# The modulation's product in column groups on TensorE, and attention steps as contiguous groups with the two heads alternating

## The chip, the core and the metric

The kernel runs on one core of one Trainium2 chip. The time is the device time of one execution in microseconds (us). Engines are named as in the profile: PE (TensorE, with its weight loads as PEld), DVE (VectorE), ACT (ScalarE), POOL (GpSimd) and SP (SyncE, which here only issues DMAs).

## What is computed

256 tokens of width 1024 pass through two hybrid layers, then through one block with modulation, two kinds of attention and a mixture of 32 experts. Cut to what matters here:

```python
for l in range(2):                                   # hybrid layers, all in float32
    h = rmsnorm(x, norm_g); proj = h @ w_in          # 1024 x 11168
    y_a = conv(...)                                  # a short causal convolution, gated
    q = (rmsnorm(c_q) @ w_uq); kv = (rmsnorm(c_kv) @ w_ukv)   # c_q 256 wide, c_kv 128 wide
    y_b = causal_attention(q, k, v) * silu(b_z)      # "mla": 8 heads
    y_c = dilated_attention(dq, dk, dv) * silu(c_z)  # "dil": 8 heads of 64, 3 groups of windows
    x = x + (g_a*(y_a @ w_out_a) + g_b*(y_b @ w_out_b) + g_c*(y_c @ w_out_c)) @ w_o

mod_x = silu(c) @ w_ada + b_ada                      # w_ada: 1024 x 6144, 25 MB
mod_c = silu(c_ctx) @ w_ada + b_ada
sh1, sc1, gt1, sh2, sc2, gt2 = split(mod_x, 6)       # of mod_c only the first two are used
h  = rms_norm(x) * (1 + sc1) + sh1                   # likewise hc from ctx with mod_c
x  = x + gt1 * (concat(gqa(h, hc), diff(h, hc)) @ w_o)   # gqa: 8 heads of 64, diff: 4 pairs of heads of 64
x  = x + gt2 * moe(rms_norm(x) * (1 + sc2) + sh2)    # 32 experts, top 4 of each token
out = rms_norm(x)
```

The modulation depends on `c` and `c_ctx` alone, so it can be worked out at any time before the second block.

## The kernel before

**Stages.** Up to some 800 us the two hybrid layers run, then the second block's attention and the router (`second`), and from about 1030 us the experts, whose 384 loads of 1 MB fill the DMA engines. All projections are float32 products made of three products of split operands (`mm3`, L180 to L182): a weight chunk of 128x4x512 (1 MB, `raw`) comes over SP's queue (L164) into a ring of three buffers with the tag `raw`; ACT makes the high part `wh` (L156), DVE the low part `wl` = `raw` − `wh` (L158); PE then multiplies the activations' parts `hh` and `hl` (or `Y`) with them. A ring buffer is free again when its `wl` is made.

**Side work.** Everything that is not a projection is written as generators: `ada` (the modulation), `mla_prep`, `mla_att`, `dil_att`, context, `gqa`, `diff`. At every weight chunk `pump` (L70) steps each generator by its rate in the table `RT` and gives its instructions the priority offset of the table `HI`. From priorities and its own estimate of time the framework's scheduler then sets the order in which each engine gets its instructions; each engine works through its own list in order, and waits at an instruction whose operand isn't there.

**The modulation (`ada`, L776).** 24 column chunks of 256, each in two halves of 512 rows: a DMA of 512 KB issued by POOL (L818), for each half. For `c`, POOL multiplies all 128x1024 numbers with silu(c) (L828) and adds them up in steps (L830, L832, L835, L836). For `c_ctx`, in the first eight chunks, DVE multiplies and adds 128x256 numbers at a time (L824, L827). What is left is summed over the 128 partitions by products with a column of ones on PE (L794 for the first eight chunks, L803 for the others). The results are `modT` (columns) and `modr` (rows).

**The attention steps.** A unit is two heads and one block of 128 queries; `pipe` alternates the first step of a unit with the second of the one before. The first makes scores for one head after the other on 64 rows of PE each (`dil` L669: three products per head of 256, 128 and 128 columns; `gqa` L958 and `diff` L986: one of 512), then the softmax; the second transposes the probabilities (`transp_p`, L599) and multiplies them with the values (L647, L684, L970, L994). In `mla_prep`, the inverse roots of four columns `css` come from `rsqrt`, eleven DVE instructions (L117 to L122). `mla_heads` scales the 128x768 queries and keys first on DVE (L478), then on POOL (L479), before rotating a part of them (L484 to L487).

## Time and profile before

| | |
|---|---|
| median of 3 runs | 1975.49 us (1973.59 to 1976.54) |
| profiled execution | 1972.42 us, its span 1970.7 us |
| PE busy | 1913.1 us (97% of the span) |
| DVE busy | 915.2 us (46%) |
| ACT busy | 615.8 us (31%) |
| POOL busy | 403.3 us (20%) |
| mean granted PE clock | 0.982 |
| DMA, mean over the span | 289 GB/s |

Busy shares are means over stages with different limits. POOL's work lies wholly ahead of the experts, and DVE's nearly so. A row of the timeline has the start, the time, the engine, the line, the output and inputs by name, the shape, the number of instructions merged in the row, and, in brackets, how long the engine stood idle ahead of it and what ended that. A float32 product shows as two instructions, its two passes. `128*64` ahead of a shape is the tile of PE that the product uses (rows*columns).

### The profile page before, as it was taken

To read this page: it belongs to the slowest core of one execution; us is meant where nothing else is said; L and a number is where in the kernel's file an instruction comes from. 1 tells how busy PE (TensorE), PEld (TensorE's weight loads), DVE (VectorE), ACT (ScalarE), POOL (GpSimd) and SP (SyncE) were. 2 spreads that over 40 slices of the span, in tenths; PEclk is the share of its full clock that TensorE was granted. 3 is DMA by queue.
4 is the path that set the end of the run, shared out by engine and by line. 5 is a ranking of instruction groups with operands and counts; after the bars stand their busy time and mean duration, and the time that the engine had idled before them with its cause. 6 is when DMAs were issued, how large, how long until landed. Compare 5 with 4: busy or idle time off the path is not lost. (4 is left out here: it accounts for less than half of the span.)

```text
span 1970.7 us, 25935 instructions
## 1 busy us (share of the span) xinstructions
PE 1913.1 (97%) x10349; PEld 1184.5 (60%) x10349; DVE 915.2 (46%) x1728; ACT 615.8 (31%) x1109; POOL 403.3 (20%) x325
## 2 busy tenths in 40 slices
PE   8989999989899999999999999999999998999997
PEld 6878988978679889886663333333333333333332
DVE  6898777588976675888671101111111011111111
ACT  4646445446465454465550000000000000100001
POOL 3125436663435334512020000000000000000000
PEclk8989999999899999999999999999999998999999
DMA  6544545546446444654469999999999999999997
GB/s 222 195 142 162 189 147 168 193 172 221 164 161 213 162 132 161 214 185 140 160 238 400 420 381 421 420 421 421 420 421 421 421 421 420 420 421 420 421 421 289
DMA packets 138452, 568.59 MB, mean 289 GB/s; under 512 B 10603, under 2 KB 16747, under 8 KB 90198
## 3 DMA queue, kind: packets, MB, share of 16 engines
q1 hardware_dynamic: 129664, 540.69, 71.0%
q0 software_dynamic: 6912, 25.17, 3.7%
q8 instruction: 83, 1.36, 0.3%
q10 hardware_dynamic: 1750, 1.03, 0.2%
q14 instruction: 43, 0.35, 0.1%
HBM read 565.79 MB, written 1.05 MB: 288 GB/s over the span
## 5 line engine op out<-in xcount | busy, mean ns | idle before, releaser
L158 DVE TENSOR_TENSOR wl<-raw,wh 128x1024 fp32r<-128x1024 f32 (+3 forms) x255 | 338.4, 1330 | 125.9 <-ACT wh L156 121.9
L156 ACT ACTIVATE wh<-raw 128x1024 fp32r<-128x1024 f32 (+3 forms) x255 | 263.0, 1035 | 226.5 <-PE mm L181 204.0
L1388 ACT ACTIVATE modr<-g 128x512 f32<-128x512 f32 x32 | 20.2, 630 | 654.4 <-DVE g L1387 654.4
L182 PE MATMUL mm<-hh,wl 128*128 128x256 f32 x768 | 220.6, 289 | 0.0
L181 PE MATMUL mm<-hl,wh 128*128 128x256 f32 x768 | 220.2, 287 | 0.0
L180 PE MATMUL mm<-hh,wh 128*128 128x256 f32 x768 | 219.8, 287 | 0.0
L1387 DVE TENSOR_SCALAR g<-mm 128x512 f32<-128x512 f32 x32 | 22.1, 692 | 407.5 <-PE mm L1377 407.5
L129 POOL TENSOR_TENSOR rm<-ss,mhalf 128x1 f32<-128x1 f32 x10 | 6.3, 631 | 959.9 <-DVE ss L128 958.0
L181 PE MATMUL mm<-wl,hh 128*128 128x512 f32 (+2 forms) x424 | 170.8, 403 | 12.0 <-DVE wl L158 12.0
L182 PE MATMUL mm<-wh,hl 128*128 128x512 f32 (+2 forms) x424 | 169.9, 401 | 2.1 <-DVE hl L216 1.3
L180 PE MATMUL mm<-wh,hh 128*128 128x512 f32 (+2 forms) x424 | 163.0, 406 | 6.8 <-ACT hh L248 3.7
L828 POOL TENSOR_TENSOR araw<-araw,tb 128x1024 f32<-128x1024 f32 x48 | 104.5, 2176 | 297.2 <-DVE part L824 123.8
L182 PEld LDWEIGHTS mm<-hh,wl 128*128 128x128 f32 x768 | 144.3, 189 | 6.4 <-issue 4.4
L180 PEld LDWEIGHTS mm<-hh,wh 128*128 128x128 f32 x768 | 144.9, 189 | 4.7 <-issue 4.2
L181 PEld LDWEIGHTS mm<-hl,wh 128*128 128x128 f32 x768 | 144.8, 188 | 3.4 <-issue 2.0
L1444 DVE TENSOR_TENSOR ys<-kaT,mm 128x512 f32<-128x512 f32 x16 | 11.0, 688 | 276.7 <-PE mm L1464 266.4
L181 PEld LDWEIGHTS mm<-wl,hh 128*128 128x128 f32 x424 | 84.6, 199 | 29.2 <-DVE wl L158 14.7
L180 PEld LDWEIGHTS mm<-wh,hh 128*128 128x128 f32 x424 | 84.1, 200 | 28.0 <-ACT hh L248 5.4
L182 PEld LDWEIGHTS mm<-wh,hl 128*128 128x128 f32 x424 | 84.2, 199 | 20.1 <-DVE hl L249 2.1
L830 POOL TENSOR_TENSOR araw<-araw 128x512 f32<-128x512 f32 x48 | 83.9, 1748 | 3.6
L1377 PE MATMUL mm<-mr,xT 128*64 128x512 f32 x328 | 77.8, 603 | 0.4 <-DMA mr<-in_w_in_dram 0.4
L1365 PEld LDWEIGHTS mm<-modr,vb 128*128 128x128 f32 x512 | 63.6, 206 | 14.4 <-issue 13.0
(450 smaller groups left out, 3579.4 us busy)
## 6 DMA issues: line engine op xcount, KB each, us to landing
raw<-in_w_in_dram SPq DMA_DIRECT2D x84, 1024.0 KB, 5.4
mr<-in_w_in_dram SPq DMA_DIRECT2D x41, 1024.0 KB, 18.2
mw<-in_w_in_dram SPq DMA_DIRECT2D x39, 1024.0 KB, 19.8
mv<-in_w_in_dram SPq DMA_DIRECT2D x27, 1024.0 KB, 19.8
mY<-in_w_in_dram SPq DMA_DIRECT2D x26, 1024.0 KB, 19.8
araw<-in_w_ada_dram POOLq DMA_DIRECT2D x48, 512.0 KB, 4.4
mw<-in_w_out_dram SPq DMA_DIRECT2D x21, 1024.0 KB, 19.2
mr<-in_w_out_dram SPq DMA_DIRECT2D x19, 1024.0 KB, 19.8
```

The lines of the kernel that those rows point to most:

```text
L156: nc.scalar.activation(wh, src, AF.Copy)
L158: eng.tensor_tensor(wl, src, wh.bitcast(F32), op=ALU.subtract)
L180: nc.tensor.matmul(out, sh, mh, start=first, stop=False, skip_group_check=skip)
L181: nc.tensor.matmul(out, sh, ml, start=False, stop=False, skip_group_check=skip)
L182: nc.tensor.matmul(out, sl, mh, start=False, stop=last, skip_group_check=skip)
L828: nc.gpsimd.tensor_tensor(raw, raw, cT[:, 0, kh * 4:kh * 4 + 4, None].to_broadcast([128, 4, 256]), op=ALU.mult)
L830: nc.gpsimd.tensor_tensor(raw[:, 0:2], raw[:, 0:2], raw[:, 2:4], op=ALU.add)
L1365: nc.tensor.matmul(p[:, j], self.h2[:, t, k * 128:(k + 1) * 128], sx[:, t].rearrange("p e c -> p (e c)"), start=(t == 0 and j == 0), stop= ...
L1377: mm = self.nc.tensor.matmul(hp[i][h * 64:h * 64 + 64], xT[:, k, cols], w[:, o:o + 512], start=False, stop=(k == 7))
L1387: nc.vector.tensor_scalar(g, hg, 7.0, None, op0=ALU.min)
L1388: nc.scalar.activation(th, g, AF.Tanh, scale=0.851)
L1444: nc.vector.tensor_tensor(ys[:, h], gt2[h], yp[h], op=ALU.mult)
```

## The change

**`ada`.** The weights come in 24 loads of 128x2048 (1 MB) by SP's queue, into the ring of the projections' chunks (the same tag and three buffers). Each load is multiplied on PE with a stationary operand of 128x32, whose first two columns are silu(c) and silu(c_ctx) and the others zero, in four products of 512 columns, each in its own group of 32 columns of PE. DVE adds the result out of PSUM to what is there (ACT copies the first). After a third, four transposes turn the first 2048 columns into `modT`. POOL's and DVE's products with the weights, the sums by ones and the column `one` go. The rate falls from 0.437 to 0.235 steps per chunk.

**Groups.** `group()` raises the priority by 400 around the transposes of `transp_p`, the products with the values and the scores, so that the scheduler keeps them together. In `dil`, `gqa` and `diff`, scores of both heads go to two PSUM tiles taken at once, with the heads alternating, so that neighbours use different halves of PE's rows.

**Two small ones.** `mla_prep` makes its inverse roots by one power on POOL; only half of `modr` is cleared at the start.

```diff
-RT = {"ada": 0.437, ...}
+RT = {"ada": 0.235, ...}
+GROUP = 400
+    def group(self):
+        return self.tc.high_priority(offset=GROUP)
...
     def mla_prep(self, l, ps):
+        r = tmp.tile([128, 4], F32, name="cr", tag="cr", bufs=1)
+        nc.gpsimd.tensor_tensor(r, css, self.mhalf, op=ALU.pow)
         yield
-        r = self.rsqrt(tmp, css, 4, "c")
...
     def transp_p(self, p, nb):
-        for j in range(nb):
-            nc.tensor.transpose(ps[:, j, :], p[:, j * 128:(j + 1) * 128], self.ident)
+        with self.group():
+            for j in range(nb):
+                nc.tensor.transpose(ps[:, j, :], p[:, j * 128:(j + 1) * 128], self.ident)
...
     def dil_att(self, l):
         def first(pr, t):
+            ss = [self.at_ps([128, 512]) for _ in range(2)]
+            with self.group():
+                for g, o, n in cols[t]:
+                    for e in range(2):
+                        es = slice(e * 64, (e + 1) * 64)
+                        nc.tensor.matmul(ss[e][:, o:o + n], self.qT[g][es, pr, ts],
+                                         self.kT[g][es, pr, ts if g else slice(0, 256)], start=True, stop=True)
             for e in range(2):
-                s = self.at_ps([128, 512])
-                for g, o, n in cols[t]:
-                    nc.tensor.matmul(s[:, o:o + n], self.qT[g][es, pr, ts], ...)
...
     def ada(self):
+        cS = A.tile([128, 8, 32], F32, name="cS", tag="cS")
+        acc = A.tile([128, 512], F32, name="aacc", tag="aacc")
+        for r in range(3):
+            dst = acc if r == 0 else self.modr[:, r - 1]
+            for kk in range(8):
+                raw = self.ring.tile([128, 2048], F32, name="araw", tag="raw")
+                nc.sync.dma_start(raw, d["w_ada"][kk * 128:(kk + 1) * 128, r * 2048:(r + 1) * 2048])
+                p = self.at_ps([128, 512])
+                with self.group():
+                    for j in range(4):
+                        nc.tensor.matmul(p[32 * j:32 * j + 32], cS[:, kk, :], raw[:, j * 512:(j + 1) * 512],
                                          start=True, stop=True)
+                if kk:
+                    nc.vector.tensor_tensor(dst, dst, p, op=ALU.add)
+                else:
+                    nc.scalar.activation(dst, p, AF.Copy)
+                yield
+            if r == 0:
+                columns()
+                yield
-        for c in range(24):
...
-                nc.gpsimd.dma_start(raw, d["w_ada"][kh * 512:(kh + 1) * 512, c * 256:(c + 1) * 256]
-                                    .rearrange("(k p) n -> p k n", p=128))
...
-                            nc.vector.scalar_tensor_tensor(parts[1], raw[:, k, :], cT[:, 1, kk:kk + 1], parts[1],
-                                                           op0=ALU.mult, op1=ALU.add)
...
-                nc.gpsimd.tensor_tensor(raw, raw, cT[:, 0, kh * 4:kh * 4 + 4, None].to_broadcast([128, 4, 256]),
-                                        op=ALU.mult)
-                nc.gpsimd.tensor_tensor(raw[:, 0:2], raw[:, 0:2], raw[:, 2:4], op=ALU.add)
```

**What it moves, in the engines' orders.** A row has the line, the instruction, output and inputs (a number behind a name is that of the buffer), the output's shape, and a count where rows repeat. The lines after the change are shifted: L180 to L182 become L184 to L186, L669 becomes L673, L164 L168, L479 L483.

PE before, at the first dilated scores of the first layer, between projection products of 256 columns:

```order
L182 MATMUL mm<-Y_99,wl 128x256
L180 MATMUL mm<-Y_99,wh 128x256
L669 MATMUL at<-kT_169,qT_166 128x128
L181 MATMUL mm<-Y_99,wh 128x256
L669 MATMUL at<-kT_170,qT_167 128x128
L182 MATMUL mm<-Y_99,wl 128x256
```

PE after, at the same unit, with a group of the modulation (L821) ahead of it:

```order
L821 MATMUL at<-araw,cS 32x512 x4
L673 MATMUL at<-kT_168,qT_165 128x256 x2
L673 MATMUL at<-kT_169,qT_166 128x128 x2
L673 MATMUL at<-kT_170,qT_167 128x128 x2
L184 MATMUL mm<-hh,wh 128x256
L185 MATMUL mm<-hl,wh 128x256
```

The scores of this unit, scattered one by one before, now stand in pairs of the two heads (x2). PE after, at the next unit, some 15 rows on:

```order
L184 MATMUL mm<-hh,wh 128x256
L673 MATMUL at<-kT_169,qT_166 128x128
L673 MATMUL at<-kT_170,qT_167 128x128
L673 MATMUL at<-kT_168,qT_165 128x256
L185 MATMUL mm<-hl,wh 128x256
L186 MATMUL mm<-hh,wl 128x256
```

Here the three products of one head stand together, but without the other head's between them, and projections follow.

POOL before, around `mla_heads` of the second layer:

```order
L818 DMA araw<-in_w_ada_dram 128x4x256
L828 TENSOR_TENSOR araw<-araw,tb 128x1024
L830 TENSOR_TENSOR araw<-araw 128x512
L479 TENSOR_TENSOR Vd<-Vd,tb 128x768 x4
L832 TENSOR_TENSOR part_5569<-araw 128x256
L818 DMA araw<-in_w_ada_dram 128x4x256
```

POOL after, the same place, from the layer's first norm (L130):

```order
L130 TENSOR_TENSOR rm<-ss,mhalf 128x1 x2
L427 TENSOR_TENSOR cr<-css,mhalf 128x4
L483 TENSOR_TENSOR Vd<-Vd,tb 128x768 x4
L506 MEMSET u 128x4x2
L832 MEMSET brow 128x1024
```

The modulation's instructions are gone from POOL, and the power of `mla_prep` (L427) stands ahead of the four products.

SP before, in the first layer:

```order
L164 DMA raw<-in_w_ukv_dram 128x512
L164 DMA raw<-in_w_in_dram 128x4x512 x17
L164 DMA raw<-in_w_out_b_dram 128x4x512
L164 DMA raw<-in_w_in_dram 128x4x512 x2
L164 DMA raw<-in_w_out_b_dram 128x4x512
```

SP after, the same stretch, up to the last of these 17 chunks but one:

```order
L168 DMA raw<-in_w_ukv_dram 128x512
L168 DMA raw<-in_w_in_dram 128x4x512 x3
L817 DMA araw<-in_w_ada_dram 128x2048
L168 DMA raw<-in_w_in_dram 128x4x512 x5
L817 DMA araw<-in_w_ada_dram 128x2048
L168 DMA raw<-in_w_in_dram 128x4x512 x4
L817 DMA araw<-in_w_ada_dram 128x2048
L168 DMA raw<-in_w_in_dram 128x4x512 x4
L817 DMA araw<-in_w_ada_dram 128x2048
```

A load of the modulation's weights now stands between every two to six chunks of the projections, in the same queue and the same ring.

## Rows read from the trace of the kernel before

**Rows 1.** Windows: stretch, width, busy PE, PEld, DVE, ACT, POOL; clock, DMA, GB/s

```profile
0.00:50.00 50.00, 40.75 (x192) 32.81 (x193) 33.51 (x60) 21.56 (x40) 16.62 (x27) 0.83 0.67 224
...
100.00:150.00 50.00, 43.44 (x198) 35.42 (x197) 46.63 (x105) 23.25 (x36) 15.93 (x10) 0.90 0.43 137
...
400.00:450.00 50.00, 44.84 (x240) 37.08 (x240) 41.69 (x47) 23.18 (x40) 29.30 (x23) 1.00 0.53 181
...
500.00:550.00 50.00, 42.16 (x192) 34.73 (x191) 45.14 (x96) 23.62 (x33) 14.13 (x6) 0.90 0.49 162
...
1200.00:1900.00 700.00, 691.58 (x3116) 266.00 (x3114) 94.42 (x154) 45.86 (x84) 0.00 (x0) 0.99 1.01 421
```

**Rows 2.** Timeline of all engines from 502 to 518 us

```profile
502.50 2.73 POOL L828 TENSOR_TENSOR araw<-araw,tb 128x1024 f32<-128x1024 f32 x1 [3.21 <-DMA araw<-in_w_ada_dram]
...
503.39 1.89 DVE L122 SCALAR_TENSOR_TENSOR rs_y<-rs_t,rs_y 128x32 f32<-128x32 f32 x1
...
505.31 1.32 DVE L120 SCALAR_TENSOR_TENSOR rs_t<-rs_y 128x32 f32<-128x32 f32 x1
...
507.81 6.80 DVE L478 TENSOR_TENSOR Vd<-Vd,rs_y 128x768 f32<-128x768 f32 x4
...
514.53 2.82 DVE L158 TENSOR_TENSOR wl<-raw,wh 128x1024 fp32r<-128x1024 f32 x1
...
517.40 0.80 PE L181 MATMUL mm<-wl,hh 128*128 128x512 f32 x1 [7.37 <-DVE wl L158]
```

**Rows 3.** Timeline of all engines from 37 to 42 us

```profile
37.87 1.88 POOL L828 TENSOR_TENSOR araw<-araw,tb 128x1024 f32<-128x1024 f32 x1 [6.19 <-DVE rs_t L120]
...
37.89 1.89 DVE L121 TENSOR_TENSOR rs_t<-rs_t,css 128x4 f32<-128x4 f32 x1
...
39.81 0.16 DVE L122 SCALAR_TENSOR_TENSOR rs_y<-rs_t,rs_y 128x4 f32<-128x4 f32 x1
...
41.40 0.45 PE L432 MATMUL at<-ident,G 128*128 128x128 f32 x1 [3.25 <-DVE G L427]
```

**Rows 4.** Timeline of all engines from 423 to 427 us

```profile
423.63 0.57 POOL L129 TENSOR_TENSOR rm<-ss,mhalf 128x1 f32<-128x1 f32 x1 [9.17 <-DVE ss L128]
...
424.18 1.88 POOL L828 TENSOR_TENSOR araw<-araw,tb 128x1024 f32<-128x1024 f32 x1
424.23 2.38 DVE L227 TENSOR_SCALAR XM<-x,rm 128x1024 f32<-128x1024 f32 x1 [0.69 <-POOL rm L129]
...
426.76 0.41 PE L243 MATMUL at<-ident,XM 128*128 128x128 f32 x2 [1.82 <-DVE XM L227]
```

**Rows 5.** Waits of PE, longest in total: us, times, longest

```profile
PE mm L181 <- DVE wl L158: 12.0, 4, 7.4
```

**Rows 6.** Timeline of PE from 961 to 1032 us

```profile
961.62 1.98 PE L986 MATMUL mm<-kbT,G 64*128 64x512 f32 x6
963.53 1.08 PE L1164 MATMUL at<-rt,sT 128*128 128x32 f32 x8
...
967.18 1.12 PE L986 MATMUL mm<-kbT,G 64*128 64x512 f32 x2
968.23 0.50 PE L180 MATMUL mm<-wh,Y 128*128 128x512 f32 x1
...
1015.72 0.43 PE L1194 MATMUL mm<-kaT,rt 128*32 128x128 f32 x8
1015.96 0.40 PE L1194 MATMUL mm<-va,rt 128*32 128x128 f32 x8
...
1017.09 1.09 PE L1341 MATMUL mm<-bi,ident 32*64 32x512 f32 x8
...
1031.09 1.08 PE L1377 MATMUL mm<-mv,xT 128*64 128x512 f32 x4
```

**Rows 7.** DMA issues: queue, count, KB each, median us to landing

```profile
raw<-in_w_in_dram SPq DMA_DIRECT2D x84, 1024.0 KB, 5.4
```

**Rows 8.** Waits of SP's queue: us, times, longest

```profile
SPq L164 <- DVE wl L158: 497.1, 80, 19.3
```

More of the change, by code (lines that the diff above doesn't have):

```diff
@@ L841, in ada, with columns @@
-        post(*last)
+        nc.vector.tensor_scalar(cS[:, :, 0:2].rearrange("p k i -> p i k"), cT, 0.5, None, op0=ALU.mult)
+        def columns():
+            p = self.at_ps([128, 4, 128])
+            for b in range(4):
+                nc.tensor.transpose(p[:, b, :], acc[:, b * 128:(b + 1) * 128], self.ident)
+            pv = p.rearrange("p b (j c) -> p j b c", j=4)
+            for v in range(2):
+                bias = self.cols[:, o + 24 + v * 8:o + 32 + v * 8].rearrange("p (j b) -> p j b", j=2)
+                for i in range(2):
+                    m = self.modT[:, v, i, :].rearrange("p (j b) -> p j b", j=2)
+                    nc.vector.tensor_tensor(m, bias, pv[:, 2 * v:2 * v + 2, :, i], op=ALU.add)
+            for i in range(2):
+                nc.vector.scalar_tensor_tensor(self.modT[:, 1, i, :], self.modT[:, 1, i, :], 1.0,
+                                               self.cols[:, o:o + 8], op0=ALU.add, op1=ALU.mult)
@@ L954, in first @@
             out = []
+            ss = [self.mm_ps([128, 512]) for _ in range(2)]
+            with self.group():
+                for e in range(2):
+                    es = slice(e * 64, (e + 1) * 64)
+                    nc.tensor.matmul(ss[e], self.qaT[es, pr, t * 128:(t + 1) * 128], self.kaT[es, :], start=True,
+                                     stop=True)
             for e in range(2):
[L956 to L959 removed]
+                p, rs = self.softmax_ps(ss[e])
                 nc.vector.tensor_scalar(p, p, rs, None, op0=ALU.mult)
@@ L966, in second @@
             o = self.o_ps([128, 128])
-            for b in range(4):
-                for e in range(2):
-                    es = slice(e * 64, (e + 1) * 64)
-                    nc.tensor.matmul(o[es], self.va[:, b, es], pT[e][:, b, :], start=(b == 0), stop=(b == 3))
+            with self.group():
+                for b in range(4):
+                    for e in range(2):
+                        es = slice(e * 64, (e + 1) * 64)
+                        nc.tensor.matmul(o[es], self.va[:, b, es], pT[e][:, b, :], start=(b == 0), stop=(b == 3))
             sl = slice(t * 128, (t + 1) * 128)
@@ L981, in first @@
         def first(t, h):
-            pp = []
-            for e in range(2):
-                es = slice(e * 64, (e + 1) * 64)
-                s = self.mm_ps([128, 512])
-                nc.tensor.matmul(s, self.qbT[es, h, t * 128:(t + 1) * 128], self.kbT[es, h, :], start=True,
-                                 stop=True)
-                pp.append(self.softmax_ps(s, raw=True))
+            ss = [self.mm_ps([128, 512]) for _ in range(2)]
+            with self.group():
+                for e in range(2):
+                    es = slice(e * 64, (e + 1) * 64)
+                    nc.tensor.matmul(ss[e], self.qbT[es, h, t * 128:(t + 1) * 128], self.kbT[es, h, :], start=True,
+                                     stop=True)
+            pp = [self.softmax_ps(s, raw=True) for s in ss]
             (p0, s0), (p1, s1) = pp
@@ L998, in second @@
             o = self.o_ps([128, 128])
-            for b in range(4):
-                nc.tensor.matmul(o, pT[:, b, :], self.vb[:, b, h * 128:(h + 1) * 128], start=(b == 0), stop=(b == 3))
+            with self.group():
+                for b in range(4):
+                    nc.tensor.matmul(o, pT[:, b, :], self.vb[:, b, h * 128:(h + 1) * 128], start=(b == 0), stop=(b == 3))
             od = tmp.tile([128, 128], F32, name="od", tag="yt", bufs=2)
```

83 lines of the change are left out of this document (17 added, 66 removed).

## Prediction

> **What bounds the kernel now.** I read the windows first. From 1200 us on the DMA engines are fully busy at 421 GB/s [rows 1]: the 384 MB of expert weights set the pace to the end. The change touches nothing there (TensorE's and SP's orders are the same in it). That part starts when TensorE is through with the router (first expert product at 1031.09 us, [rows 6]), so a microsecond won before it moves the end by one. Before it TensorE is the bound: most windows have it busy throughout, and the idle time lies in a few, of which [rows 1] shows four: 9.2 us in 0 to 50, 6.6 in 100 to 150, 5.2 in 400 to 450, 7.8 in 500 to 550. In three of these the granted clock is below 1 as well (0.83, 0.90, 0.90), between its levels 1.2 and 2.4 GHz: after a wait the products run at the lower level for a while, so a wait costs more than itself.
>
> Then I asked who ends these waits. The list of waits names VectorE: L181 waits for `wl`, 12.0 us in four waits, the longest 7.4 [rows 5]; and so do the single waits of L432 for L427 [rows 3] and of L243 for L227 [rows 4]. The reader should ask next why VectorE is late, and the timeline says it: VectorE's instructions are stretched beside GpSimd's. At 37.89 a product of 128x4 elements takes 1.89 us, as long as the 1.88 us of GpSimd's L828, which began 0.02 us earlier; the next instruction of the same chain takes 0.16 [rows 3]. At 424.23 L227 takes 2.38 us beside an L828 of 1.88 [rows 4]. At 503.39 and 505.31 two instructions of 128x32 take 1.89 and 1.32 us beside L828 and the L830 that follows it [rows 2]. So the modulation's product on GpSimd, which nothing needs soon, takes time from VectorE, and VectorE's delay reaches TensorE.
>
> **What the change takes away.** All L828 and the additions behind them leave GpSimd, whose order falls from 396 rows to 173. What of it reaches TensorE, place by place:
>
> a) 500 to 550. VectorE loses 1.89 + 1.32 − 2 x 0.16 = 2.9 us ahead of L478, and PE's wait of 7.37 us ends with the `wl` right behind L478 [rows 2]: the wait falls to some 4.5 us. It does not go, since L478 (6.80 us for its four products) and the `wl` behind it (2.82) run beside GpSimd's L479, which stays. The first layer has the same place near 100 us. With the same share (2.9 of 7.4) 4.7 us of the 12.0 us of L181's waits go. The clock: a mean of 0.90 over 50 us means 10 us at the lower level in each window, so some 5 us lost in each; the same share of both is 3.9 us. Sum 8.6 us; the low end is 4.7, the waits alone.
>
> b) 37 us. `rsqrt` of four columns, eleven VectorE instructions in a chain, becomes one power on GpSimd; such a power takes 0.57 us for one column [rows 4], on an engine that has nothing else then. L121's 1.89 us beside L828 goes, and with the chain L432's wait of 3.25 us [rows 3]. With the slow products behind the wait I take 4 us; from 0 (another operand just as late) to 5.
>
> c) 400 to 450. L243 waits 1.82 us for L227, stretched by L828 [rows 4]; GpSimd is busy 29 of these 50 us [rows 1], so I put most of the window's other waits to the same cause and take 4 of its 5.2 us; the low end is the 1.8.
>
> Sum 16.6 us; by the ends 6.5 to 18.8.
>
> **What it adds on TensorE.** Two places give the prices. At 961.62 three products of L986 (two passes each; float32, 512 columns, 64 rows) take 1.91 us to the next instruction, two of them running together in the two halves of the rows; at 967.18 one alone takes 1.05 us [rows 6]. So the cost of going over to another tile size and back is 0.19 us for each change counted, and two passes take 0.86 us: 2 x 0.86 + 0.19 = 1.91 and 0.86 + 0.19 = 1.05. A pass scales with its columns. Column tiles run together too: eight instructions on four tiles of 128x32 with 128 columns start 0.24 us before the next eight [rows 6], where two passes of 128 columns alone would take 0.22.
>
> A group of the modulation thus takes 0.86 us. In the order 18 of the 24 stand whole and 6 are broken in two: 30 sets, 25.8 us. The four transposes add 0.4. Gone are L803 (16 products of 256 columns, 2 x 0.215 us each, 6.9 us) and L794 (64 short instructions, taken as passes of 128 columns, 0.11 us each, 7.0 us). The dilated scores are 32 products of 256 and 64 of 128 columns on 64 rows, in 96 sets before: 32 x 0.43 + 64 x 0.22 = 28.2 us. In the order 73 sets are left (whole groups would give 48; many are still cut by projections): 21.8 us, 6.4 less. GQA's scores go from 12 to 14 sets (1.7 more), the differential ones from 13 to 12 (0.9 less), the products with V and the transposes add 1.6. Changes of tile size fall from 333 to 290: 43 x 0.19 = 8.2 us less. Sum: 25.8 + 0.4 − 6.9 − 7.0 − 6.4 + 1.7 − 0.9 + 1.6 − 8.2 = 0.1 us. TensorE has as much work as before; what is won is in the waits.
>
> Of a group 512 columns wide on 128 rows, no row here tells. The Trainium skill, "TensorE: Matmul & The Clock Gate", section "Measured speedup vs the span model", has 3.07 times for four row tiles of 512 columns and 2.38 for three column tiles, not 4 and 3. By that a group would take 4 x 0.86/3.07 = 1.12 us, an estimate, and the sum would be 7.8 us worse.
>
> VectorE gets 21 additions out of PSUM for 64 short instructions that leave it, ScalarE three copies: both have room, and I cost them at nothing.
>
> **What it adds on SP and in the ring.** The 24 loads of 1 MB go through SP's queue now and take one of the ring's three `raw` buffers each. SP waits 497 us, in 80 waits, for a `wl` to free such a buffer [rows 8]: loads go out as early as buffers allow, and mostly well ahead of their use. A load takes 5.4 us [rows 7]. A group stands in PE's queue in front of projections, so if its load is late, all behind it wait. In the order 13 of the 24 loads are issued with only 4.6 to 7.4 us of PE's work left before their group, the other 11 with 13 or more. Against 5.4 us that is about even, and it is the buffers' release, not PE, that these loads follow. I take 0 as the value, and 0.8 us for each of the 13 (10 us) as the bad end.
>
> **Result.** The profiled execution took 1972.4 us; less 16.6 and plus 0.1 that is 1955.9. The median of the runs lies 3.1 above it, so 1975.5 − 16.5 = 1959.0 us is what I expect to be measured.
>
> **The rivals.**
> 1) *The ring starves PE* (slower). It turns on one number, by how much the average `araw` lands after PE has come to its group: at 0.69 us (16.5/24) the gain is gone, at 1.6 us 38 us are added and the time is 1997 us (1959 + 38). For it: there are still three buffers, 13 loads have little lead, and while an `araw` sits in one, the projections have two. Against it: by 5.4 us of landing and 2.8 of the slowest split in [rows 2], two buffers still bring a chunk every 4.1 us, while TensorE uses 138 chunks in 1030 us, one per 7.5; and the DMA engines are only 0.43 to 0.67 busy in the windows before 550 us [rows 1]. Chance 0.10.
> 2) *The waits only change their owner* (no change): L478 beside L479 stays, and behind `wl` a `wh` or a load may be late by as much. 1975 us, within 4. Against it: in [rows 2] and [rows 3] the operand that came last is the one behind VectorE's stretched chain. Chance 0.12.
> 3) *The column groups run less together* (less gain). L1341's eight instructions of 512 columns on four tiles take 1.09 us [rows 6], 0.23 more than 0.86, though the tail of the last is in it. With this for each of the 30 sets 6.9 us are lost: 1965.9 us. Against it: the 0.24 us of the 128-column tiles leave about 10%, not 27%. Chance 0.15. The page named above speaks for this case.
> 4) *The change doesn't bring the groups that it says*: the order answers this, 6 broken groups and 73 sets for 48, which is in the sum; no chance of its own.
> 5) *More waits go than I count*: the 7.3 us of L181's waits that a) leaves, with the rest of the clock (6 us), because L479 starts without L828 ahead of it and is through sooner, and all of c): 1944 us. Chance 0.13.
>
> My forecast, 1952 to 1964 us, has 0.50.
>
> **How the numbers follow.** Faster by over 0.2% (about 4 us, what a measurement here can tell from no change) holds the forecast and the rivals 3 and 5: 0.78. Within 0.2%: 0.12. Slower: 0.10. The range takes in most of rivals 2 and 5 and leaves out rival 1: 1941 to 1975 us.
>
> **What would show it.** In the profile of the changed kernel: no VectorE instruction of 128x4 or 128x32 above 0.3 us but beside L479 (now L483); PE idle under 7 us in 0 to 50 and under 2 in 400 to 450; the wait near 510 us at 4 to 5 us, ended by `wl` again; a group's four tiles starting within 0.05 us of each other, 0.43 us a pass; the first expert product near 1014 us instead of 1031. Wrong would be: PE waiting at L821 for `araw`, above 15 us in all (rival 1); the wait near 510 us still at 7 us, or ended by ScalarE (rival 2); passes of a group 0.55 us apart (rival 3).

## The result, and the profile after

The changed kernel takes 1947.18 us (median of four runs, 1945.82 to 1949.04) against 1974.92 us for the kernel before in the same series: the ratio is 0.9858, with a 95% interval of 0.9836 to 0.9879. 27.7 us were won where 16.5 were forecast (1959.0 us); the time lies in the range (1941 to 1975 us) and 4.8 us under the band of 1952 to 1964 us that I held likeliest.

The profiled execution of the changed kernel took 1947.53 us. The experts' first product starts at 1008.01 us, 23.1 us earlier than in [rows 6]:

```profile
1008.01 1.94 PE L1371 MATMUL mm<-mv,xT 128*64 128x512 f32 x8
```

From there to the end it is 937.8 us, before it was 939.6. All kernels of this study, with the same work in this stage, have 937.8 to 940.0 us, so these 2 us come and go without the change. What has to be explained are the 23 us.

**Is it TensorE's work or its waits?** The prediction priced every product in TensorE's order (two passes of 512 columns 0.86 us, 0.19 us for each change of tile size, from [rows 6]). Summed over all that stands ahead of the experts, that is 974.9 us before and 974.8 us after. What is left up to the first expert product is time in which TensorE waited or ran at its lower clock, called waits below: 1031.1 − 974.9 = 56.2 us before, 1008.0 − 974.8 = 33.2 us after. By this sum all 23 us are waits and none is work.

That is a remainder, so it needs a second source. The trace itself has PE idle for 37.8 us up to the first expert product before and for 24.4 after. The mean granted clock there rises from 0.979 to 0.992; counted as (1 − clock) times the stretch, the time lost at the lower level falls from 22.2 to 8.5 us. Together that is 60.0 and 32.9 us, where the remainder has 56.2 and 33.2; in all 14 kernels the two agree within 4 us. So the waits fall by 23 to 27 us, about half of it as idle time and half as clock, and TensorE's work is the same within 4 us. Both counts are made for each experiment below.

The windows (columns as in [rows 1]) show where the time went, the list of PE's waits who ended them:

```profile
0.00:50.00 50.00, 45.42 (x243) 38.05 (x244) 27.34 (x45) 27.59 (x50) 3.40 (x18) 0.97 0.69 231
...
100.00:150.00 50.00, 47.36 (x230) 38.47 (x230) 39.28 (x117) 29.40 (x49) 0.00 (x0) 0.97 0.50 165
400.00:450.00 50.00, 48.35 (x286) 42.10 (x285) 29.51 (x44) 25.26 (x46) 2.57 (x3) 1.00 0.53 182
475.00:525.00 50.00, 46.53 (x214) 38.20 (x213) 43.94 (x100) 26.01 (x37) 10.21 (x4) 0.97 0.53 173
500.00:550.00 50.00, 49.46 (x248) 40.24 (x249) 39.76 (x128) 30.70 (x55) 0.11 (x1) 1.00 0.53 173
```

```profile
PE mm L185 <- DVE wl L162: 8.2, 5, 2.5
...
PE at L247 <- DVE XM L231: 1.4, 2, 0.9
```

PE's idle time falls from 9.2 to 4.6 us in 0 to 50 and from 5.2 to 1.7 in 400 to 450; the place near 510 us has moved to 490. The clock is at 0.97 or more where it was 0.83 and 0.90. GpSimd has little left to do: 3.4 us of the first 50 where it had 16.6. The `wl` waits (L185, before L181) fall from 12.0 us with a longest of 7.4 to 8.2 with a longest of 2.5.

The place of [rows 2], all engines, in the changed kernel (L482 was L478, L483 was L479):

```profile
484.97 6.88 DVE L482 TENSOR_TENSOR Vd<-Vd,rs_y 128x768 f32<-128x768 f32 x4
...
491.78 2.84 DVE L162 TENSOR_TENSOR wl<-raw,wh 128x1024 fp32r<-128x1024 f32 x1
```

```profile
486.10 10.21 POOL L483 TENSOR_TENSOR Vd<-Vd,tb 128x768 f32<-128x768 f32 x4 [60.66 <-DVE Vd L482]
```

```profile
494.68 0.50 PE L185 MATMUL mm<-wl,hh 128*128 128x512 f32 x1 [2.21 <-DVE wl L162]
```

The pair of VectorE and GpSimd instructions takes as long as before (6.88 us beside 10.21), and so does the `wl` behind it. But VectorE comes to it 7.5 us before PE runs dry (494.68 − 2.21 − 484.97), where it was 2.2 us (517.40 − 7.37 − 507.81 in [rows 2]): the wait shrinks by the 5.2 us that VectorE's lead has grown, not by the 2.9 us that I saw in the instructions right ahead of it. The kernel before has two more stretched instructions on VectorE, ahead of the place where [rows 2] begins:

```profile
492.09 1.34 DVE L121 TENSOR_TENSOR rs_t<-rs_t,dss 128x16 f32<-128x16 f32 x1
...
494.49 1.25 DVE L122 SCALAR_TENSOR_TENSOR rs_y<-rs_t,rs_y 128x16 f32<-128x16 f32 x1
```

With the two of [rows 2] the four take 5.8 us, where such an instruction takes 0.16 to 0.19 us unstretched: about 5.1 us, the size of the lost lead. From 490.1 us to L478 the trace names no idle time of VectorE in which to make it up.

The place of [rows 3]: the power on GpSimd, and what waits for it.

```profile
26.71 1.02 POOL L427 TENSOR_TENSOR cr<-css,mhalf 128x4 f32<-128x4 f32 x1 [18.23 <-DVE css L425]
```

```profile
28.83 0.35 DVE L431 TENSOR_SCALAR G<-G,cr 128x256 f32<-128x256 f32 x1
```

```profile
31.75 0.49 PE L436 MATMUL at<-ident,G 128*128 128x128 f32 x3
```

L436 (before L432) has no wait in its brackets any more; the first scaled part of `G` is there 2.6 us before.

A group of the modulation on PE, whole and broken:

```profile
56.65 0.40 PE L184 MATMUL mm<-wh,hh 128*128 128x512 f32 x1
56.98 1.06 PE L821 MATMUL at<-araw,cS 128*32 128x512 f32 x8
57.98 0.51 PE L185 MATMUL mm<-wl,hh 128*128 128x512 f32 x1
```

```profile
247.01 1.05 PE L821 MATMUL at<-araw,cS 128*32 128x512 f32 x2
247.98 1.15 PE L673 MATMUL at<-kT,qT 64*128 64x256 f32 x12
249.06 1.06 PE L821 MATMUL at<-araw,cS 128*32 128x512 f32 x6
250.05 0.39 PE L184 MATMUL mm<-hh,wh 128*128 128x256 f32 x1
```

Eight instructions take 1.00 us from the first one's start to the next product's, a change of tile size in part included; in the trace the four tiles start 5 to 7 ns apart and the second pass 454 ns after the first. A broken part of a group costs as much with one product (0.97 us) as with three (0.99).

The waits of SP's queue, and what ended PE's idle time ahead of L821:

```profile
SPq L168 <- DVE wl L162: 361.9, 65, 12.1
...
SPq L817 <- DVE wl L162: 89.0, 16, 10.8
...
SPq L168 <- PE at L821: 70.3, 18, 15.1
```

```profile
its engine sat idle before it (us, times) until:
  issue: 2.7, 11
  PE at L475: 0.2, 1
  PE at L247: 0.2, 1
```

No DMA stands there (the 2.7 us of `issue` are time for which the profile shows no cause): PE did not wait for a load of the modulation. SP's waits are of the same size in sum as in [rows 8] (362 + 89 + 70 us, before 497), only the ring buffers are now freed by groups too.

### The profile page after: what moved, and what is told of

The parts are those of the page before. It is cut to its first block, busy times and chain, and to the rows that moved or that the text cites. A ratio compares the mean times of both kernels' runs of the same rounds, so it can differ in the third digit from the quotient of the medians.

```text
span 1945.9 us, 25819 instructions
## 1 busy us (share of the span) xinstructions
PE 1899.4 (98%) x10449; PEld 1165.6 (60%) x10449; DVE 818.3 (42%) x1651; ACT 611.3 (31%) x1096; POOL 99.7 (5%) x111
## 5 line engine op out<-in xcount | busy, mean ns | idle before, releaser
L162 DVE TENSOR_TENSOR wl<-raw,wh 128x1024 fp32r<-128x1024 f32 (+3 forms) x255 | 312.5, 1227 | 188.9 <-ACT wh L160 181.7
L184 PE MATMUL mm<-hh,wh 128*128 128x256 f32 x768 | 219.1, 286 | 0.0
L186 PE MATMUL mm<-hh,wl 128*128 128x256 f32 x768 | 218.5, 286 | 0.0
L185 PE MATMUL mm<-hl,wh 128*128 128x256 f32 x768 | 218.2, 285 | 0.0
L185 PE MATMUL mm<-wl,hh 128*128 128x512 f32 (+2 forms) x424 | 168.2, 398 | 8.2 <-DVE wl L162 8.2
L186 PE MATMUL mm<-wh,hl 128*128 128x512 f32 (+2 forms) x424 | 167.0, 394 | 0.5 <-DVE hl L253 0.4
L184 PE MATMUL mm<-wh,hh 128*128 128x512 f32 (+2 forms) x424 | 159.9, 399 | 4.0 <-ACT hh L252 2.5
L184 PEld LDWEIGHTS mm<-hh,wh 128*128 128x128 f32 x768 | 144.8, 189 | 7.1 <-issue 6.5
L186 PEld LDWEIGHTS mm<-hh,wl 128*128 128x128 f32 x768 | 144.1, 188 | 5.8 <-issue 5.4
L185 PEld LDWEIGHTS mm<-hl,wh 128*128 128x128 f32 x768 | 144.7, 188 | 3.5 <-issue 3.4
L185 PEld LDWEIGHTS mm<-wl,hh 128*128 128x128 f32 x424 | 83.3, 196 | 25.2 <-DVE wl L162 10.2
L184 PEld LDWEIGHTS mm<-wh,hh 128*128 128x128 f32 x424 | 82.2, 196 | 19.9 <-ACT hh L252 3.3
L186 PEld LDWEIGHTS mm<-wh,hl 128*128 128x128 f32 x424 | 83.3, 196 | 17.1 <-issue 2.4
L1371 PE MATMUL mm<-mw,xT 128*64 128x512 f32 x312 | 72.0, 594 | 0.0
L1335 PE MATMUL mm<-bi,ident 32*64 32x512 f32 x256 | 65.3, 627 | 4.6 <-PEq L1478 4.6
L1359 PE MATMUL mm<-modr,vb 128*128 128x128 f32 x512 | 65.5, 289 | 0.0
```

Source lines behind the costliest of these rows:

```text
L162: eng.tensor_tensor(wl, src, wh.bitcast(F32), op=ALU.subtract)
L184: nc.tensor.matmul(out, sh, mh, start=first, stop=False, skip_group_check=skip)
L185: nc.tensor.matmul(out, sh, ml, start=False, stop=False, skip_group_check=skip)
L186: nc.tensor.matmul(out, sl, mh, start=False, stop=last, skip_group_check=skip)
L1335: self.nc.tensor.matmul(hp[h * 64:h * 64 + 64], oh(i).to_broadcast([32, 64]), self.bi[32 + 32 * i:64 + 32 * i, h * 512:(h + 1) * 512], sta ...
L1359: nc.tensor.matmul(p[:, j], self.h2[:, t, k * 128:(k + 1) * 128], sx[:, t].rearrange("p e c -> p (e c)"), start=(t == 0 and j == 0), stop= ...
```

## The experiments

Twelve kernels were run, each timed beside the kernel before, whose median was 1973.5 to 1976.3 us in these series. In the table, work and waits are the two parts of the time up to the first expert product, as above (the work from the kernel's own order, the product from its trace). The last column is the second count: PE's idle time plus the time lost at the lower clock, from the trace alone.

| kernel | median, us | ratio to before, 95% | first expert product | TensorE's work | waits | idle + clock |
|---|---|---|---|---|---|---|
| before | 1974.9 | | 1031.1 | 974.9 | 56.2 | 37.8 + 22.2 |
| changed | 1947.2 | 0.9836 to 0.9879 | 1008.0 | 974.8 | 33.2 | 24.4 + 8.5 |
| e1_ada | 1973.0 | 0.9986 to 1.0010 | 1036.3 | 1001.9 | 34.4 | 24.1 + 8.5 |
| e2_groups | 1976.3 | 0.9994 to 1.0018 | 1034.5 | 962.4 | 72.1 | 51.4 + 22.2 |
| e3_pow | 1970.0 | 0.9963 to 0.9988 | 1024.7 | 973.7 | 51.0 | 38.7 + 13.7 |
| e4_quiet | 1958.7 | 0.9892 to 0.9944 | 1018.5 | 975.8 | 42.7 | 29.6 + 13.7 |
| e5_pool_reads | 1979.3 | 1.0016 to 1.0044 | 1037.5 | 974.8 | 62.7 | 40.6 + 18.8 |
| e6_pool_writes | 1949.9 | 0.9858 to 0.9902 | 1008.0 | 974.8 | 33.2 | 24.1 + 8.5 |
| e7_nogroup | 1996.0 | 1.0074 to 1.0133 | 1059.1 | 1017.5 | 41.6 | 29.2 + 13.7 |
| e9_heads | 1946.3 | 0.9832 to 0.9880 | 1007.2 | 975.1 | 32.1 | 23.6 + 10.2 |
| e10_groups_quiet | 1941.0 | 0.9804 to 0.9839 | 1002.8 | 961.0 | 41.8 | 29.1 + 11.9 |
| e11_heads_prio | 1947.0 | 0.9839 to 0.9880 | 1004.2 | 974.0 | 30.2 | 25.2 + 5.1 |
| e12_whole | 1941.5 | 0.9815 to 0.9863 | 1001.3 | 970.3 | 31.0 | 24.6 + 6.8 |
| e13_both | 1938.0 | 0.9796 to 0.9848 | 998.2 | 968.6 | 29.6 | 23.9 + 5.1 |

### Was it GpSimd's reading beside VectorE? (e5, e6)

Two kernels give GpSimd back about as much work as the modulation was (390 and 331 us busy, before 403), but work that nothing waits for, behind each group of the changed kernel: one reads and writes SBUF with arithmetic, the other only writes.

The reads (`cb` is silu(c), spread over 128x4x256):

```diff
+                nc.scalar.activation(scr[:, 0, 0:1], p[:, 0:1], AF.Copy)
+                for _ in range(2):
+                    nc.gpsimd.tensor_tensor(scr, scr, cb, op=ALU.subtract)
+                    nc.gpsimd.tensor_tensor(scr[:, 0:2], scr[:, 0:2], scr[:, 2:4], op=ALU.subtract)
+                    nc.gpsimd.tensor_tensor(scr[:, 0], scr[:, 0], scr[:, 1], op=ALU.subtract)
+                    nc.gpsimd.tensor_tensor(scr[:, 0], scr[:, 0], scr[:, 1], op=ALU.subtract)
```

The writes:

```diff
+                nc.scalar.activation(scr[:, 0, 0:1], p[:, 0:1], AF.Copy)
+                for _ in range(10):
+                    nc.gpsimd.memset(scr, 1.0)
```

> The changed kernel with arithmetic on GpSimd that nothing needs: behind each of the 24 groups eight instructions on a scratch tile that read and write SBUF, in the sizes of the modulation's before (128x1024, 128x512, twice 128x256, all twice), some 9 us per group, 220 us in all, and a copy of 128x1 on ScalarE that starts them. TensorE's order has the same work and changes of tile size as the changed kernel's. Theory (VectorE loses time to GpSimd's reads beside it): VectorE's instructions of 128x4 to 128x32 are stretched to 1 to 2 us again, 1957 to 1972 us. Rival (the gain came from the loads, the queue or VectorE's lighter list): 1947 us, as the changed kernel.

> The same with GpSimd's reads taken out: ten memsets of the scratch tile of 128x1024 per group, 0.94 us each, so as much busy time on GpSimd, in the same place, but instructions that only write. Theory (it is the reading beside VectorE that costs): as the changed kernel, 1947 us within 4. Rival (any work of GpSimd on SBUF costs VectorE): as the kernel with the reads, 1957 to 1972 us.

With the reads 1979.3 us, with the writes 1949.9: 29.4 us apart, with the same work on PE. The changed kernel's whole gain goes with the reads, and somewhat more (I had expected 1957 to 1972 us), while the writes are within the 4 us that were named. The rows of `wl`, which takes more of VectorE's time than any other line (e5, then e6), and the window of 400 to 450 us (same order):

```profile
L162 DVE TENSOR_TENSOR wl<-raw,wh 128x1024 fp32r<-128x1024 f32 (+3 forms) x255 | 339.6, 1334 | 148.7 <-ACT wh L160 147.5 <-PE mm L185 0.3
```

```profile
L162 DVE TENSOR_TENSOR wl<-raw,wh 128x1024 fp32r<-128x1024 f32 (+3 forms) x255 | 312.9, 1229 | 174.9 <-ACT wh L160 173.4 <-PE mm L185 0.6
```

```profile
400.00:450.00 50.00, 40.84 (x217) 33.19 (x215) 38.42 (x40) 20.23 (x39) 28.49 (x20) 0.93 0.46 152
```

```profile
400.00:450.00 50.00, 48.51 (x287) 42.32 (x286) 30.88 (x44) 25.94 (x48) 21.75 (x23) 1.00 0.53 180
```

GpSimd is busy 28 and 22 of these 50 us (in e5 its own instructions are stretched too). Beside its reads VectorE takes 38.4 us for 40 instructions, beside its writes 30.9 for 44, and PE has 9.2 us idle against 1.5.

A rival is that the added work blocks something else: ScalarE's small copy waits for GpSimd's added work (6.2 us in all in e5, 1.5 in e6), and could hold up PE. It doesn't decide. Up to the first expert product, PE's idle time ended by ScalarE is 10.1 us in both kernels; that ended by VectorE is 28.6 us in e5 and 12.2 in e6 (23.4 before, 12.9 in the changed kernel). PE's largest wait (e5, then e6):

```profile
PE mm L185 <- DVE wl L162: 12.8, 13, 2.4
```

```profile
PE mm L185 <- DVE wl L162: 8.0, 5, 2.5
```

So it is shown that GpSimd's arithmetic on SBUF makes VectorE, and through it PE, late, and that GpSimd's being busy is not enough for it. What the two runs part is arithmetic that reads and writes from writing alone; no run has reading by itself. The Trainium skill, "SBUF — State Buffer", section "Who interferes with whom", says that a VectorE instruction with two inputs in SBUF contends with a GpSimd instruction that reads SBUF, not with one that only writes it. These two runs agree with it (29.4 us apart). One row goes further than the sentence: L227 in [rows 4], with one such input, was stretched too, to 2.38 us where the same instruction takes 0.75 at 7.69 us; the same section has that for instructions in a mode that takes both port pairs, and which mode L227 ran in no row tells.

### The halves of the change alone (e1, e2, e3)

e1 is the changed kernel with `mla_prep`, `transp_p` and the scores and products of all four attentions taken back:

```diff
-        r = tmp.tile([128, 4], F32, name="cr", tag="cr", bufs=1)
-        nc.gpsimd.tensor_tensor(r, css, self.mhalf, op=ALU.pow)
         yield
+        r = self.rsqrt(tmp, css, 4, "c")
...
-        with self.group():
-            for j in range(nb):
-                nc.tensor.transpose(ps[:, j, :], p[:, j * 128:(j + 1) * 128], self.ident)
+        for j in range(nb):
+            nc.tensor.transpose(ps[:, j, :], p[:, j * 128:(j + 1) * 128], self.ident)
...
```

> The modulation's new product alone: column groups and loads through the ring as in the changed kernel, while transposes, scores, products with the values and the inverse roots of mla_prep are as before. Counted from its order, with 0.19 us per change of tile size (333 of them before, 418 here), TensorE has 27 us more to do than before. Theory (GpSimd's arithmetic was what made VectorE late): waits of TensorE ahead of the experts fall from 56 to 33 to 40 us as in the changed kernel, so 1975 + 27 - 16 to 23 = 1979 to 1986 us. Rival (the gain came from the groups of the attention): waits stay at 56 us, 2002 us.

Its waits are 34.4 us, the lower end of what the theory gave, and its time of 1973.0 us lies under the 1979 to 1986 us that I made of it. The modulation's move alone brings the waits down, with VectorE's chain of `rsqrt` still in it. But TensorE has 27 us more to do, since the groups' tile size stands among single attention products (418 changes of size for 333). By the profile the experts start 5.2 us later than before; the medians are 1.7 us lower, which the runs don't tell from nothing.

e2 is the kernel before with the changed kernel's attention, that is `group()` around transposes, scores and products, and the alternating heads; `ada` and `mla_prep` are as before:

```diff
+GROUP = 400
...
+    def group(self):
+        return self.tc.high_priority(offset=GROUP)
...
+        with self.group():
+            for j in range(nb):
+                nc.tensor.transpose(ps[:, j, :], p[:, j * 128:(j + 1) * 128], self.ident)
...
```

> The attention's groups and alternating heads alone; the modulation on GpSimd and the inverse roots on VectorE as before. By its order TensorE has 12.5 us less to do (284 changes of tile size for 333, 3 us less of products). Theory: the waits behind GpSimd's arithmetic stay at 56 us, so 1975 - 12.5 = 1962 us, and the wait behind L478 near 500 us is still above 6 us. Rival (fewer changes of tile size are eaten by waits): 1970 to 1975 us.

It missed: 1976.3 us. TensorE has 12.5 us less to do, and 15.9 us more of waits took that. These rows name the largest new one (PE, ACT, POOL):

```profile
406.96 0.80 PE L184 MATMUL mm<-wh,hh 128*128 128x512 f32 x1 [7.25 <-ACT hh L219]
```

```profile
406.28 0.63 ACT L219 ACTIVATE hh<-M 128x512 fp32r<-128x512 f32 x1 [11.90 <-POOL M L582]
```

```profile
401.80 1.88 POOL L837 TENSOR_TENSOR araw<-araw,tb 128x1024 f32<-128x1024 f32 x1 [3.41 <-DMA araw<-in_w_ada_dram]
403.76 1.26 POOL L839 TENSOR_TENSOR araw<-araw 128x512 f32<-128x512 f32 x1
404.98 2.49 POOL L582 TENSOR_TENSOR M<-M,th 128x512 f32<-128x512 f32 x2
```

PE waits for `hh`, ScalarE for `M`, and GpSimd's `M` (L582) stands in its queue behind the modulation's L837, which itself waits for its load. So the modulation on GpSimd cost in a second way as well: as a queue. A second new wait is for the modulation itself, GpSimd's `part`:

```profile
254.47 0.58 PE L803 MATMUL at<-tb,part 128*128 128x1 f32 x2 [3.38 <-POOL part L845]
```

The wait for `wl` behind L482 is that of before (7.2 us).

> The attention's groups alone, as in e2_groups, on a kernel before whose GpSimd does none of the modulation's arithmetic, as in e4_quiet (ScalarE passes the first loaded 256 columns on in its place; the sums it stands for are left out). By its order TensorE has 961.0 us to do ahead of the experts, 13.9 less than before. Theory (e2's groups do save TensorE's time, and waits behind GpSimd's multiplications ate it): waits fall from e2's 72 us to 33 to 43, first expert product near 994 to 1004 us, 1934 to 1944 us. Rival (the groups bring waits of their own, whatever GpSimd does): waits at 55 us or more, 1956 us or more.

e10 takes GpSimd's arithmetic out of e2 and settles it: 1941.0 us, the waits fall by 30 us to 41.8, and the 13.9 us that TensorE has less to do come out in the time. Neither half does without the other: the groups give nothing while PE waits on GpSimd, and the modulation's move costs 27 us of PE's time without the groups, 12 to 14 with them (974.8 − 962.4 = 12.4, and 1.2 more if the power's saving in e3's order is taken out).

e3 changes `mla_prep` alone:

```diff
+        r = tmp.tile([128, 4], F32, name="cr", tag="cr", bufs=1)
+        nc.gpsimd.tensor_tensor(r, css, self.mhalf, op=ALU.pow)
         yield
-        r = self.rsqrt(tmp, css, 4, "c")
```

> Only the inverse roots of mla_prep as a power on GpSimd; all else as before. Theory: the 3.3 us wait near 38 us and the slow products behind it go (4 to 7 us), and TensorE's order has 1.2 us less: 1966 to 1970 us. Rival: GpSimd's queue has the modulation's multiplications ahead of the power, the wait stays or gets longer: 1974 to 1980 us.

1970.0 us, the end of what was expected. The window that held the wait of 3.25 us in [rows 3] has PE busy again, at the full clock (before, then e3):

```profile
25.00:50.00 25.00, 21.68 (x132) 19.39 (x131) 19.77 (x34) 10.26 (x21) 11.73 (x9) 0.86 0.60 194
```

```profile
25.00:50.00 25.00, 24.66 (x165) 23.37 (x164) 19.40 (x26) 14.54 (x27) 15.51 (x10) 1.00 0.62 207
```

In the changed kernel, though, the power is not what this window needed: e1, which keeps the chain, has no idle time of PE there either, since with the modulation gone from GpSimd and VectorE its chain is through by 30.3 us, where it took until 40.0 before.

### GpSimd's arithmetic alone taken away (e4)

```diff
-                nc.gpsimd.tensor_tensor(raw, raw, cT[:, 0, kh * 4:kh * 4 + 4, None].to_broadcast([128, 4, 256]),
-                                        op=ALU.mult)
-                nc.gpsimd.tensor_tensor(raw[:, 0:2], raw[:, 0:2], raw[:, 2:4], op=ALU.add)
...
+                    nc.scalar.activation(parts[0], raw[:, 0], AF.Copy)
                     yield
```

> The kernel before with GpSimd's multiplications and additions of the modulation left out (for c the first loaded 256 columns are passed on in their place, copied by ScalarE); GpSimd still issues the 48 loads, VectorE's products for c_ctx and TensorE's sums stay. TensorE's order has 0.9 us more. Theory: waits fall from 56 us to some 33 as in the changed kernel: 1975 - 22 = 1950 to 1957 us. Rival (the waits have other causes, such as the loads or VectorE's own work for the modulation): 1968 us or more.

1958.7 us, 16 us less than before: 13.5 us of waits go, where I expected some 20 and 1950 to 1957 us. From 50 to 550 us, which has the waits behind L478 and the one for L227, idle time and lost clock fall from 30.3 to 13.2 us; the changed kernel has 13.5. There GpSimd's arithmetic is the whole cause. PE's waits ended by VectorE fall from 23.4 to 10.9 us.

What this kernel doesn't gain lies in the first 50 us, 16.3 us lost against 17.8 before and 6.3 in the changed kernel. Part of it is the experiment's own doing. The chain of `rsqrt` is through 5 us earlier and L432 no longer waits for it; but the copy L829, put in for this run, waits for its load on ScalarE, and `Y` stands behind it in ScalarE's list (PE, ACT, PE):

```profile
37.31 0.82 PE L432 MATMUL at<-ident,G 128*128 128x128 f32 x6
```

```profile
40.19 0.42 ACT L829 ACTIVATE part<-araw 128x256 f32<-128x256 f32 x1 [1.25 <-DMA araw<-in_w_ada_dram]
```

```profile
41.02 0.69 PE L180 MATMUL mm<-wh,Y 128*128 128x384 f32 x1 [2.89 <-ACT Y L435]
```

So the 13.5 us are a lower bound for what GpSimd's arithmetic costs before. They can't be added to the 5 us of e3, since both take away the wait of L432. The other part is the start: in the first 25 us this kernel loses 10.0 us, before 11.0, e1 and the changed kernel 6.4 and 6.3. That difference is not GpSimd's arithmetic; it went in e1 and the changed kernel, where the modulation's loads by GpSimd and VectorE's products for `c_ctx` are gone from the start as well.

### What the groups are worth (e7)

```diff
     def group(self):
-        return self.tc.high_priority(offset=GROUP)
+        return ExitStack()
```

> The changed kernel with group() doing nothing: heads still alternate, the modulation is still on TensorE, but the scheduler gives no priority to groups. By its order TensorE has 42.7 us more (387 changes of tile size for 290, and 24 us more of products that no longer stand beside one that they could run with). Theory (TensorE's own work is the bound, its sum as I count it): 1947 + 43 = 1986 to 1992 us. Rival (part of it falls into waits that are there anyway): 1960 to 1975 us.

1996.0 us, 48.8 us above the changed kernel and above the 1986 to 1992 us expected; 42.7 had been counted as work, and 8 us of waits came with it. TensorE's work can be read off its order: 59 sets of modulation products in place of 30, 387 changes of tile size in place of 290.

### What is left in the changed kernel (e9, e11, e12, e13)

What waits stay in the changed kernel? Near 94 and 492 us, `wl` behind L482 beside GpSimd's L483. e9 takes that pair away:

```diff
-                nc.vector.tensor_tensor(s, s, mr[:, i, t, :, None].to_broadcast([128, 8, 96]), op=ALU.mult)
-                nc.gpsimd.tensor_tensor(s, s, self.ggq[:, l, i, None, :].to_broadcast([128, 8, 96]), op=ALU.mult)
+                for h in range(8):
+                    nc.vector.scalar_tensor_tensor(s[:, h, :], s[:, h, :], mr[:, i, t, h:h + 1], self.ggq[:, l, i, :],
+                                                   op0=ALU.mult, op1=ALU.mult)
```

> The changed kernel with the scaling of queries and keys (L482 on VectorE, then L483 on GpSimd) made by one instruction per head on VectorE, eight of 128x96 for each of the four in a layer; GpSimd's L483 is gone. TensorE's order has 0.3 us more. Theory: the waits near 97 and 102 us and near 494 us (2.2, 2.5, 2.2, 1.0 us, with slow products behind them, 11 to 12 us in all) come from L482 and wl beside L483 and go: 1935 to 1941 us. Rival (the eight short instructions take VectorE as long as the stretched L482 did): 1945 to 1949 us.

1946.3 us: no gain that can be told. VectorE is through sooner, 21 of the 32 instructions in 4.91 us, and nothing is stretched, but PE's next step now waits:

```profile
480.94 4.91 DVE L483 SCALAR_TENSOR_TENSOR Vd<-Vd,rs_y,tb 128x96 f32<-128x96 f32 x21
```

```profile
490.81 1.05 PE L475 MATMUL at<-ident,Vd 128*96 128x128 f32 x8 [2.43 <-DVE dss L135]
492.84 0.80 PE L185 MATMUL mm<-wl,hh 128*128 128x512 f32 x1 [0.99 <-DVE wl L162]
```

The wait has changed its owner, from `wl` to the heads' transposes (L475), as in the prediction's second rival. In 450 to 550 us PE's idle time is 3.4 us with e9 and was 3.5 in the changed kernel. In 50 to 150 us it falls from 4.9 to 2.4 us, L475 being the owner there too, but 2.0 us of a new wait for `wl` stand near 799 us.

```diff
-HI = {..., "prep": 0, ...}
+HI = {..., "prep": -40, ...}
```

> e9_heads (scaling of the heads by one instruction per head on VectorE) with the priority offset of mla_prep's work lowered from 0 to -40, below that of wl (-30), so that VectorE makes a chunk's wl ahead of the 32 short instructions where both are ready. TensorE's order has 974.0 us, 0.8 less than the changed kernel's. Theory (the wait of the second layer near 490 us is VectorE's order of work): the 5 us of waits left there fall to 1 or 2, 1938 to 1942 us. Rival (the attention's start then waits for mla_prep instead): 1945 to 1950 us.

1947.0 us, the time that the rival gave, though the experts start 3.8 us earlier than in the changed kernel by the profile; 3.1 us of wait for `wl` stay near 494 us, the only wait of PE in 450 to 550 us, so the rival's reason, an attention that waits for `mla_prep`, doesn't show there. These two don't beat the changed kernel by more than their runs scatter.

The other thing left is TensorE's work: six broken groups of the modulation.

```diff
-                with self.group():
+                with self.tc.high_priority(offset=1000):
                     for j in range(4):
                         nc.tensor.matmul(p[32 * j:32 * j + 32], cS[:, kk, :], raw[:, j * 512:(j + 1) * 512],
```

> The changed kernel with the modulation's groups at a priority offset of 1000, above the 400 of the other groups. In its order all 24 groups are whole (18 before, 6 broken by dilated scores); TensorE has 4.5 us less to do, all in products, the changes of tile size stay at 290. Theory (TensorE is the bound and the broken groups cost 0.86 us each): 1943 us, first expert product 4 to 5 us earlier, if the waits stay at 33 us. Rival (waits take it up): 1947 us.

1941.5 us (1939.8 to 1943.8): 5.7 us under the changed kernel, with no run as slow as its fastest. The kernel before was 1.2 us faster in this series than in the changed kernel's, so by the ratios (0.9839 against 0.9858) it is some 4 us. By the profile the first expert product is 6.7 us earlier: 4.5 us are PE's work, 2.2 us fewer waits.

> e12_whole together with e11_heads_prio (the heads scaled on VectorE alone, mla_prep's priority at -40). TensorE's order has 968.6 us to do, 6.2 less than the changed kernel's. Theory (TensorE's work plus the 30 us of waits of e11): first expert product near 999 us, 1938 to 1941 us. Rival: waits grow as the work shrinks, 1944 to 1947 us.

1938.0 us (0.9822 of before, 0.9796 to 0.9848) is the fastest kernel here, 9.2 us below the changed one, some 7 by the ratios, whose intervals still touch. By the profile 6.2 us are work and 3.6 us waits.

## Why the prediction was right, point by point

**What bounds.** Right: TensorE up to the experts, DMA behind it, and a microsecond won ahead of the experts is one at the end: in all 14 kernels the stage of the experts takes 937.8 to 940.0 us.

**TensorE's work: 0.1 us more by the sum, and the trace agrees within 4 us.** Taking PE's idle time and the lost clock off the time up to the first expert product leaves 971.1 us of work before and 975.1 after. For e7 it gives 41 us more than for the changed kernel, where the order had 42.7, and for e12 5.3 less, where it had 4.5. The group was priced at 0.86 us; its two passes take 0.91 (454 ns each), which is 1.5 us of the 4 over 30 sets; the rest is open. One term doesn't follow from its prices: the dilated scores before, 32 x 0.43 + 64 x 0.22, are 27.8 us, not 28.2, so the sum would be 0.5. The third rival (27% more for a group) is out: the four tiles run 3.8 times as fast as one after the other (4 x 0.43/0.454), not 3.07, the figure that the Trainium skill, "TensorE: Matmul & The Clock Gate", section "Measured speedup vs the span model", has for four row tiles, nor in the proportion of its three column tiles.

**The cause of the waits.** Right for most of them: GpSimd's arithmetic beside VectorE, by e4, e5 and e6. The start of the kernel has another cause, which the prediction didn't have.

**Where the size was off.** The sum of waits that go was put at 16.6 us; it measured 23.0 as a remainder (56.2 to 33.2) and 27.1 by idle time and clock (60.0 to 32.9). That is why the time came out under the likeliest band. It lies in the range because the range was drawn to take in most of the fifth rival. By the terms, in idle time and lost clock:

- *a)* 50 to 150 and 450 to 550 us: 8.6 us forecast, 25.1 − 11.8 = 13.3 measured. I took 2.9 of 7.4 us as the share, from the two stretched instructions right ahead of L478. What counts is VectorE's lead over PE, and with it the four stretched instructions since VectorE last stood idle: 5.2 us.
- *b)* The chain of `rsqrt`, 25 to 50 us: 4 us forecast, 6.7 measured, because the slow products behind the wait came to 3.4 us where I allowed 0.8. The power was not needed for it: e1 gets the same without.
- The start, 0 to 25 us: nothing forecast, 11.0 − 6.3 = 4.7 measured. e4 keeps most of this loss (10.0), so it isn't GpSimd's arithmetic. The first weights come earlier without the modulation's loads beside them (ScalarE's first `wh` starts at 9.19 us in place of 11.16, in e4 at 10.87); no run parts this from VectorE's products for `c_ctx`.
- *c)* 400 to 450 us: 4 forecast, 5.2 − 1.6 = 3.6 measured.
- Behind 800 us the waits grew by 1.3 us, which no term had.

*a)* and *b)* erred in the same way: I priced each stall by what stood right ahead of it or by the wait alone, and left out the lost lead further back and the slow products behind.

**The ring.** I took 0 for the loads with little lead, and no wait of PE for `araw` shows. The loads land in 5.0 us (median) where I had 5.4, and even the 13 with 4.6 to 7.4 us of lead were in time. With how little to spare, no run tested.

**The second rival**, that waits change their owner, did not decide here, but it did in e2 (PE waits behind GpSimd's queue, which eats what its shorter work would win) and in e9.

**The signs named ahead.** VectorE's instructions of 128x4 to 128x32, with inputs as narrow, above 0.3 us: 18 before, one after (0.90 us at 1002 us, beside GpSimd's L1273 and not L483), so right but for one. PE idle below 7 us in 0 to 50 (4.6) and below 2 in 400 to 450 (1.7): right. Near 510 us, 4 to 5 us of wait ended by `wl`: ended by it, but 2.2 and 1.0. Tiles within 0.05 us and 0.43 us a pass: 0.02 and 0.454, so right and 6% more. First expert product near 1014: 1008.

**The fifth rival** (more waits go) was the nearest to what came: its reason, that L479 starts earlier and is through sooner, was wrong, for the pair takes as long as before (6.88 and 10.21 us); what moved was when VectorE gets there.

## What to carry to other kernels

Before moving arithmetic to an idle GpSimd, look at VectorE's short instructions beside it in the timeline: where they take as long as GpSimd's, the engine isn't free, and work that only writes, or none, is what fits there. Price such a contention by the lead that it takes from VectorE since VectorE last stood idle, not by the stretched instructions next to the wait: e5, whose stretched instructions at 474.8 to 482.1 us lie ahead of idle time of VectorE (1.00 us at 503), has the full lead of 7.5 us at this place. Look also at what an experiment puts in place of the work that it takes out: e4's copy brought a wait of its own. Small tile sizes pay on TensorE only where they stand together: the modulation's products cost 27 us among single attention products and 12 to 14 beside groups, so group first, and then see which waits eat the gain.

## What I had not expected of the hardware

- GpSimd's memsets in e6 (GpSimd is busy 331 us in all, 231 more than in the changed kernel) cost nothing that can be told (1949.9 against 1947.2 us, the first expert product within 0.1 us); arithmetic that reads and writes in their place (390 us, 290 more, part of it because GpSimd's instructions are stretched as well, 128x1024 from 1.9 up to 3.0 us) cost 29 us more.
- Four column tiles of 128x32, 512 columns wide, in float32, run one pass in 454 ns with starts 5 to 7 ns apart, where one tile takes 430.
- A power of 128x4 on GpSimd takes 1.02 us, of 128x1 0.57 ([rows 4]).
